# A hybrid retention and attention decoder on one core: column pairs' additions split up, partly given to accumulating DMAs, and an earlier rotary chain

## The chip, the cores and the metric

The kernel runs on one core of a Trainium2 chip. The core has TensorE (PE, matmuls and transposes, with weight loads shown as PEld), VectorE (DVE), ScalarE (ACT) and GpSimd (POOL). SyncE (SP) issues most DMAs. The on-chip memories are SBUF and, for matmul results, PSUM. The metric is the device time of one execution in microseconds (us), lower is better.

## The reference

Two decoder layers work on 256 positions of width 2048, all in fp32. Layer 0 is a retention layer with eight heads, layer 1 is multi-head latent attention (MLA) with 16 heads. Each is followed by a squared-ReLU MLP of width 8192.

```python
for layer in range(DEPTH):
    if layer < N_A_LAYERS:
        h = rms_norm(x, norm_mix[layer])
        x = x + retention(h, ret_w_in[layer], ret_w_out[layer], ret_cos, ret_sin)
    else:
        ...  # shared keys and values once, from the stream after layer 0
        x = x + mla_attention(h, mla_w_dq[j], ..., k_nope, k_pe, v, mla_cos, mla_sin)
    x = x + sq_relu_mlp(rms_norm(x, norm_mlp[layer]), mlp_w1[layer], mlp_w2[layer])

def sq_relu_mlp(h, w1, w2):
    return jnp.square(jax.nn.relu(h @ w1)) @ w2
```

In retention, queries and keys are rotated by tables of sines and cosines of position times frequency:

```python
def rope_tables(positions, dim):
    inv_freq = 1.0 / (ROPE_BASE ** (jnp.arange(0, dim, 2, dtype=jnp.float32) / dim))
    ang = positions.astype(jnp.float32)[..., None] * inv_freq
    return jnp.cos(ang), jnp.sin(ang)
```

## The kernel before

**Matmuls.** Each fp32 operand is split into a high and a low part (`split`, lines 149 to 158). ACT casts the high part, DVE subtracts to get the low part. Three matmuls (high by high, high by low, low by high) make one fp32 product. Weights stream through SBUF in chunks of 1 MB: SP issues the load into one of three `raw` buffers, then ACT and DVE split it in halves into five `wh` and five `wl` buffers, and PE multiplies.

**The program order and the planner.** The Python code runs the steps of a matrix product one chunk at a time. Each chunk ends with `tick()`, which advances a clock by one. Other work is put in a queue with `later(n, fn)` and is written out when the clock reaches its due time (lines 78 to 96). `need` runs queued work early when a list must already have entries. The framework's planner then lays out each engine's instructions, those earlier in program order first where several are ready by its estimates, and adds the waits. On the chip, each engine takes its instructions strictly in that order. SBUF tiles come from small pools; the general pool `f2k` has 14 buffers of 2 KB per partition.

**The start.** The eight halves of the first gate product load their weights and inputs step by step (`start`, lines 539 to 552). After half 3, positions, constants and `gpe` are loaded on SP's queue. After half 5, `ret_tables` (lines 501 to 503) casts the positions on DVE and calls `sincos`, a chain of POOL instructions that reduces the angles to the range of the sine table. `scale_tables` (lines 505 to 515) takes the sine on ACT, multiplies by the row scales of x, and has PE transpose the result (`tr_tp`) into `rope_tab`, with which head 0's queries and keys are rotated.

**The MLP.** The hidden width is worked on in four groups (`mlp`, lines 670 to 726). Of each group there are two up products (`u`) and two down products (`d`) by column pairs of 1024 columns. A column pair (`gemm_pair`) takes eight chunks, called row pairs or quads here, since each holds a 2 by 2 arrangement of blocks. Five quads do eight block products. Three of them, numbers 3, 5 and 7, do seven block products with sums of the weight blocks and of the inputs; DVE makes these sums, so such a quad has fewer matmuls (21 instead of 24) and more DVE work. The seven-product sums end in the PSUM tiles p1, p5, p6 and p7. `pair_out` (lines 332 to 345) brings a pair to its end: six copies by ACT and eight additions by DVE.

For an up pair, `up` (lines 678 to 698) applies the ReLU, and one step later `turn` transposes on PE (`hid_tp`), squares, and splits, which makes four blocks of hidden inputs. For a down pair, `add` (lines 716 to 723) sends four POOL DMAs that accumulate the result into x's home in DRAM (`x_home`). In the last group, the first down pair is instead added to x in SBUF by `done` (`into_next` in layer 0, `finish` in layer 1, both through `add_to_x`, line 415). The last two column blocks then come by plain products (`d_acc`).

**Attention.** After the queries of a block, `query`, `score` and `values` follow one another through `later`. `values` (lines 952 to 959) multiplies by V on PE (`ao`), one step after the transposes of the probabilities are written out (line 948).

Lines that matter below:

```python
                queue.append((clock[0] + 1, -1, lambda: done(pair_out(made, name))))   # 329
        for key, add in (("c11", o["p1"]), ("c12", v), ("c21", u), ("c22", o["p5"])):  # 343
            nc.vector.tensor_tensor(o[key], o[key], add, op=ALU.add)                   # 344
                later(1, turn)                                                         # 698
                            nc.gpsimd.dma_start(x_home[t][b], c[t][j], accum_op=ALU.add)  # 723
            later(1, lambda: values(b, pt))                                            # 948
```

Of the kernel before, what the change touches and what calls it, by code (L numbers as in the profile page):

```python
# [21 lines left out]
NT = 2  # L22
# [28 lines left out]
def yoco(ctx: ExitStack, tc: tile.TileContext, a):  # L51
# [55 lines left out]
    nc.gpsimd.memset(neg_half, -0.5)  # L107
    warm = small(1, "warm")
    nc.scalar.copy(warm, neg_half[:, 0:1])

    dram = ctx.enter_context(tc.tile_pool(name="dr", bufs=1, space=bass.MemoryType.DRAM))
    x_home = [[dram.tile([P, 512], F32, name=f"xh_{t}_{b}") for b in range(NB)] for t in range(NT)]
# [185 lines left out]
    def gemm_pair(w, chunk0, act, kinds, name, done):  # L298

        made = {}  # L300
        total, count = {}, {}
        for seven in kinds:
            for key in ("c11", "c12", "c21"):
                total[key] = total.get(key, 0) + (1 if seven else 2)
            for key in ("p1", "p5", "p6", "p7") if seven else ("c22", "c22"):
                total[key] = total.get(key, 0) + 1

        def get(key):
            if key not in made:
                if key in ("p6", "p7"):  # L310
                    both = two_banks(f"{name}_p67")
                    made["p6"], made["p7"] = both[:, 0], both[:, 1]
                else:
                    made[key] = bank("tp" if key[0] == "p" else "acc", [512], f"{name}_{key}")
            return made[key]

        def mm(key, lhs, rhs):
            dst, n = get(key), count.get(key, 0)
            count[key] = n + 1
            (ah, al), (bh, bl) = lhs, rhs  # L320
            nc.tensor.matmul(dst, ah, bh, start=n == 0, stop=False)  # L321
            nc.tensor.matmul(dst, ah, bl, start=False, stop=False)  # L322
            nc.tensor.matmul(dst, al, bh, start=False, stop=n == total[key] - 1)  # L323

        for i in range(len(kinds)):
            need(act, i + 1)
            quad(w, chunk0 + i, act[i], mm, f"{name}{i}")
            if i == len(kinds) - 1:
                queue.append((clock[0] + 1, -1, lambda: done(pair_out(made, name))))
            tick()  # L330

    def pair_out(c, name):

        o = {}
        for key in ("c22", "c12", "c11", "c21", "p1", "p5"):
            o[key] = f2k([512], f"{name}_{key}")
            nc.scalar.copy(o[key], c[key])
        v, u = (f2k([512], f"{name}_{i}") for i in "vu")
        nc.vector.tensor_tensor(v, c["p6"], o["p1"], op=ALU.add)
        nc.vector.tensor_tensor(u, c["p7"], v, op=ALU.add)  # L340
        nc.vector.tensor_tensor(v, o["p5"], v, op=ALU.subtract)
        nc.vector.tensor_tensor(o["p5"], o["p5"], u, op=ALU.subtract)
        for key, add in (("c11", o["p1"]), ("c12", v), ("c21", u), ("c22", o["p5"])):
            nc.vector.tensor_tensor(o[key], o[key], add, op=ALU.add)
        return [[o["c11"], o["c12"]], [o["c21"], o["c22"]]]

    def with_sums(blocks, name):

# [65 lines left out]

    def add_to_x(acc, b, ss, name):
        for t in range(NT):
            nc.vector.tensor_tensor(x[t][b], acc[t], x[t][b], op=ALU.add)
            if ss is not None:
                square_sum(x[t][b], ss[t][:, b : b + 1], f"{name}_{t}{b}")

# [117 lines left out]

    def start(half):
        first_inputs(half)  # L540
        if half == 3:
            nc.sync.dma_start(pos_i, a["pos"])
            nc.sync.dma_start(cst, a["cst"])
            nc.sync.dma_start(gpe, a["gpe"])
        if half == 5:
            ret_tables()
        if half == 7:
            for b in range(NB):
                later(2 + b, lambda b=b: load_x(b))
            later(5, scale_tables)  # L550
            later(12, lambda: mla_sc.append(sincos(cst[:, C_INVM : C_INVM + 32], 32, "tm")))
            later(20, mla_tables)
# [117 lines left out]
    def mlp(layer, act, r, done):  # L670
        w1, w2 = a[f"mlp_w1_{layer}"], a[f"mlp_w2_{layer}"]
        f0 = 0
        for gi, nf in enumerate(GROUPS):
            hid, blocks = [], []
            kinds = [i in SEVEN for i in range(2 * nf)]
            last = gi == len(GROUPS) - 1

            def up(c, p, hid=hid, blocks=blocks):

                need(r, NT)  # L680
                for t in range(NT):
                    for i in range(2):
                        nc.scalar.activation(c[t][i], c[t][i], AF.Relu, scale=r[t])

                def turn():
                    for q in range(4):
                        name = f"hid{layer}_{p}{q}"
                        tp = transposed(
                            lambda t, j: c[t][q // 2][:, (q % 2 * 2 + j) * P : (q % 2 * 2 + j + 1) * P], f"{name}_tp"
                        )  # L690
                        u = f2k([2, S], f"{name}_u")
                        nc.scalar.activation(u, tp, AF.Square)
                        v = act_tile(name)
                        split_act(v, u)
                        blocks.append((v, with_sums(u, name) if len(blocks) in SEVEN else None))
                        hid.append(v)

                later(1, turn)

            for p in range(f0 // 2, (f0 + nf) // 2):  # L700
                gemm_pair(
                    w1, p * 8, act, [i in SEVEN for i in range(8)], f"u{layer}_{p}", lambda c, p=p, up=up: up(c, p)
                )
            if last:
                x_tiles(lambda t, b: x_home[t][b], f"mlp{layer}")
            for p in range(2):
                if last and p:
                    for b in (2, 3):
                        need(hid, 2 * nf)
                        gemm(  # L710
                            a[f"mlp_w2t_{layer}"], (b - 2) * nf, hid, 4 * nf, 512, f"d{layer}_{gi}{b}",
                            lambda acc, b=b: done(b, acc),
                        )
                    continue

                def add(c, p=p, last=last):
                    for j in range(2):
                        b = 2 * p + j
                        if last:
                            done(b, [c[t][j] for t in range(NT)])  # L720
                            continue
                        for t in range(NT):
                            nc.gpsimd.dma_start(x_home[t][b], c[t][j], accum_op=ALU.add)

                gemm_pair(w2, p * 32 + 2 * f0, blocks, kinds, f"d{layer}_{gi}{p}", add)
            f0 += nf
# [174 lines left out]
    def score(b, qt, qpe):  # L901
# [37 lines left out]
        def turn():  # L939
            pt = []  # L940
            for hh in range(2):
# [3 lines left out]
                o = f2k([3 * P], f"pt{b}{hh}")  # L945
                nc.scalar.copy(o, tp)
                pt.append(o)
            later(1, lambda: values(b, pt))

        later(3, turn)  # L950

# [113 lines left out]
```

## Time and profile before

| what | value |
|---|---|
| median of three runs | 2537.88 us (2533.21 to 2538.45) |
| the profiled execution | 2535.52 us, span of its instructions 2533.7 us |
| mean granted clock of PE | 0.996 |
| PE busy | 2504.2 us, 99% |
| DVE busy | 1912.6 us, 75% |
| ACT busy | 1442.1 us, 57% |
| POOL busy | 180.2 us, 7% |
| moved by DMA | 501.08 MB, mean 198 GB/s |

The page gives busy time by engine. Times in the timeline are microseconds from the first instruction. A row of the timeline has its start, its length, the engine, the line in the kernel, the operation, what it writes and reads, the shapes, the count, and in brackets the idle time of the engine before it with what ended it. A row of the waits has who waited, for whom, the total, the count and the longest. A row of the windows has the stretch, its length, busy time (and count) of PE, PEld, DVE, ACT and POOL, the granted clock, the mean busy share of the 16 DMA engines, and GB/s. A row of the DMA issues has the count, the KB of each and the median time from issue to landing.

### The profile page before, as it was taken

The page shows a single profiled execution, that of the slowest core. Times are in us where ns is not written, and L with a number is a line of the kernel's source. Part 1 is how long each engine was busy: PE and PEld are TensorE (multiplying, and loading weights), DVE is VectorE, ACT ScalarE, POOL GpSimd, SP SyncE. Part 2 cuts the span into 40 slices and gives each one's busy share as a digit, 9 for nine tenths or more (in the row PEclk, how much of TensorE's full clock was granted, in tenths as well). Part 3 has the DMA queues.
Part 4 walks back from the last instruction along what each step waited for, and adds up shares of the span by engine and source line. Part 5 has one row for each costly group of instructions (what it writes and reads, how often), then busy time and mean ns, then how long its engine had stood idle before and what let it go on. Part 6 is the DMA issues. An engine that isn't in the chain of part 4 may idle for free.

```text
span 2533.7 us, 31133 instructions
## 1 busy us (share of the span) xinstructions
PE 2504.2 (99%) x11794; PEld 2092.5 (83%) x11794; DVE 1912.6 (75%) x2478; ACT 1442.1 (57%) x1993; POOL 180.2 (7%) x235
## 2 busy tenths in 40 slices
PE   8999999999999999999999999999999999999998
PEld 6888888888888888788788788998888887888887
DVE  6555555554558888889898756886688889898885
ACT  6444444444446656656566666555566566575663
POOL 6200000000000000000010101110000100000100
PEclk9999999999999999999999999999999999999999
DMA  8455555565665575665675564444655756656754
GB/s 302 165 178 183 185 173 194 174 215 184 206 204 181 189 233 199 215 217 183 218 247 185 203 207 170 162 146 166 197 185 199 233 199 199 224 191 205 261 183 150
DMA packets 82966, 501.08 MB, mean 198 GB/s; under 512 B 9856, under 2 KB 11008, under 8 KB 29568
## 3 DMA queue, kind: packets, MB, share of 16 engines
q1 hardware_dynamic: 71280, 471.78, 53.3%
q0 software_dynamic: 11392, 27.27, 5.0%
q8 instruction: 92, 1.51, 0.2%
q14 instruction: 58, 0.48, 0.1%
q10 hardware_dynamic: 144, 0.05, 0.0%
HBM read 478.09 MB, written 20.97 MB: 197 GB/s over the span
## 4 chain that ended last, share of the span: by engine, by line
PE 73%; DVE 16%; ACT 5%; issue 2%; POOL 2%; DMA 2%; SPq 0%; ACTq 0%; DVEq 0%; POOLq 0%
DVE d_wl L153 7%; PE u_c L322 6%; PE u_c L323 6%; PE u_c L321 6%; PE ro_acc L215 2%; PE ro_acc L214 2%; PE ro_acc L213 2%; PE rv_acc L215 2%; PE rv_acc L213 2%; PE rv_acc L214 2%; ACT d_wh L152 2%; PE rk_acc L241 2%; PE rq_acc L241 2%; PE d_c L322 2%; PE rg_acc L215 2%
## 5 line engine op out<-in xcount | busy, mean ns | idle before, releaser
L153 DVE TENSOR_TENSOR u_wl<-u_raw,u_wh 128x1024 fp32r<-128x1024 f32 (+1 forms) x256 | 278.7, 1118 | 25.7 <-ACT u_wh L152 25.1
L153 DVE TENSOR_TENSOR d_wl<-d_raw,d_wh 128x1024 fp32r<-128x1024 f32 (+1 forms) x256 | 282.1, 1130 | 20.6 <-ACT d_wh L152 20.2
L322 PE MATMUL u_c<-u_wl,n 128*128 128x512 f32 x736 | 287.6, 391 | 0.3 <-DVE u_wl L153 0.2
L321 PE MATMUL u_c<-u_wh,n 128*128 128x512 f32 x736 | 287.4, 390 | 0.0
L323 PE MATMUL u_c<-u_wh,n 128*128 128x512 f32 x736 | 286.4, 389 | 0.0
L152 ACT CAST d_wh<-d_raw 128x1024 fp32r<-128x1024 f32 (+1 forms) x256 | 239.5, 988 | 61.2 <-DMA d_raw<-in_mlp_w 29.9
L152 ACT CAST u_wh<-u_raw 128x1024 fp32r<-128x1024 f32 (+1 forms) x256 | 238.2, 978 | 60.5 <-PE u_c L323 37.0
L322 PE MATMUL d_c<-d_wl,hid 128*128 128x512 f32 x644 | 253.4, 393 | 4.2 <-DVE d_wl L153 4.2
L323 PE MATMUL d_c<-d_wh,hid 128*128 128x512 f32 x644 | 251.0, 390 | 0.0
L321 PE MATMUL d_c<-d_wh,hid 128*128 128x512 f32 x644 | 247.7, 391 | 0.0
L152 ACT CAST u_wh<-u_u 128x1024 fp32r<-128x1024 f32 x96 | 96.6, 1048 | 180.3 <-DVE u_u L286 164.4
L152 ACT CAST d_wh<-d_u 128x1024 fp32r<-128x1024 f32 x84 | 84.0, 1048 | 148.9 <-DVE d_u L286 145.4
L322 PEld LDWEIGHTS u_c<-u_wl,n 128*128 128x128 f32 x736 | 138.2, 188 | 29.5 <-DVE u_wl L153 1.6
L321 PEld LDWEIGHTS u_c<-u_wh,n 128*128 128x128 f32 x736 | 138.2, 188 | 28.5
L323 PEld LDWEIGHTS u_c<-u_wh,n 128*128 128x128 f32 x736 | 138.2, 188 | 28.4
L153 DVE TENSOR_TENSOR u_wl<-u_u,u_wh 128x1024 fp32r<-128x1024 f32 x96 | 113.9, 1222 | 55.0 <-ACT u_wh L152 55.0
L322 PEld LDWEIGHTS d_c<-d_wl,hid 128*128 128x128 f32 x644 | 120.9, 188 | 35.4 <-DVE d_wl L153 8.6
L321 PEld LDWEIGHTS d_c<-d_wh,hid 128*128 128x128 f32 x644 | 120.9, 188 | 25.3
L153 DVE TENSOR_TENSOR ro_wl<-ro_raw,ro_wh 128x1024 fp32r<-128x1024 f32 x64 | 78.4, 1225 | 82.2 <-ACT ro_wh L152 81.9
L323 PEld LDWEIGHTS d_c<-d_wh,hid 128*128 128x128 f32 x644 | 121.0, 188 | 23.3
L153 DVE TENSOR_TENSOR d_wl<-d_u,d_wh 128x1024 fp32r<-128x1024 f32 x84 | 99.2, 1222 | 49.7 <-ACT d_wh L152 49.7
L153 DVE TENSOR_TENSOR rg_wl<-rg_raw,rg_wh 128x1024 fp32r<-128x1024 f32 (+1 forms) x68 | 78.8, 1162 | 63.5 <-ACT rg_wh L152 63.5
(373 smaller groups left out, 6196.5 us busy)
## 6 DMA issues: line engine op xcount, KB each, us to landing
u_raw<-in_mlp_w SPq DMA_DIRECT2D x128, 1024.0 KB, 5.0
d_raw<-in_mlp_w SPq DMA_DIRECT2D x112, 1024.0 KB, 4.9
rv_raw<-in_ret_w_gv SPq DMA_DIRECT2D x32, 1024.0 KB, 4.8
ro_raw<-in_ret_w_out SPq DMA_DIRECT2D x32, 1024.0 KB, 4.9
rg_raw<-in_ret_w_gv SPq DMA_DIRECT2D x28, 1024.0 KB, 4.8
uq_raw<-in_mla_w_uq SPq DMA_DIRECT2D x24, 768.0 KB, 4.3
rq_raw<-in_ret_w_qk SPq DMA_DIRECT2D x16, 1024.0 KB, 4.8
rk_raw<-in_ret_w_qk SPq DMA_DIRECT2D x16, 1024.0 KB, 4.9
```

The lines of the kernel that those rows point to most:

```text
L152: nc.scalar.copy(h, src)
L153: nc.vector.tensor_tensor(l, src, h.bitcast(F32), op=ALU.subtract)
L213: nc.tensor.matmul(acc[t], ah, rh, start=k == 0, stop=False)
L214: nc.tensor.matmul(acc[t], ah, rl, start=False, stop=False)
L215: nc.tensor.matmul(acc[t], al, rh, start=False, stop=k == nk - 1)
L241: nc.tensor.matmul(acc[f], wh[:, cols], a.rearrange("p i s -> p (i s)"), start=k == 0, stop=k == nk - 1)
L321: nc.tensor.matmul(dst, ah, bh, start=n == 0, stop=False)
L322: nc.tensor.matmul(dst, ah, bl, start=False, stop=False)
L323: nc.tensor.matmul(dst, al, bh, start=False, stop=n == total[key] - 1)
```

## The change

- **Start.** Positions and the first 160 columns of `cst` (the frequencies) are loaded by two POOL DMAs at the very beginning. `ret_tables` is called after half 0. The rest of `cst` (mask and identity) and `gpe` are loaded by SP after half 7.
- **Column pairs.** `pair_out` makes its six copies and two additions, and puts a function `rest` in the queue, one row pair later. `rest` makes two more additions and calls `done` with pairs of addends that are not yet added.
- **Up pairs** add them in `summed`, four additions, and transpose in two batches, `turn(0)` in the same step and `turn(1)` one step later.
- **Down pairs** of the first three groups send one accumulating DMA for each addend, eight for a pair. In the last group, block 0 goes to `done` at once and block 1 two steps later, and `add_to_x` adds both addends to x one after the other.
- **Attention.** `values` is due two steps after the transposes, not one.

```diff
@@ -107,6 +107,8 @@
     nc.scalar.copy(warm, neg_half[:, 0:1])
+    nc.gpsimd.dma_start(pos_i, a["pos"])
+    nc.gpsimd.dma_start(cst[:, :C_MASK], a["cst"][:, :C_MASK])
@@ -326,10 +328,10 @@
             if i == len(kinds) - 1:
-                queue.append((clock[0] + 1, -1, lambda: done(pair_out(made, name))))
+                queue.append((clock[0] + 1, -1, lambda: pair_out(made, name, done)))
             tick()
-    def pair_out(c, name):
+    def pair_out(c, name, done):
@@ -338,11 +340,20 @@
         nc.vector.tensor_tensor(v, c["p6"], o["p1"], op=ALU.add)
         nc.vector.tensor_tensor(u, c["p7"], v, op=ALU.add)
-        nc.vector.tensor_tensor(v, o["p5"], v, op=ALU.subtract)
-        nc.vector.tensor_tensor(o["p5"], o["p5"], u, op=ALU.subtract)
-        for key, add in (("c11", o["p1"]), ("c12", v), ("c21", u), ("c22", o["p5"])):
-            nc.vector.tensor_tensor(o[key], o[key], add, op=ALU.add)
-        return [[o["c11"], o["c12"]], [o["c21"], o["c22"]]]
+
+        def rest():
+            nc.vector.tensor_tensor(v, o["p5"], v, op=ALU.subtract)
+            nc.vector.tensor_tensor(o["p5"], o["p5"], u, op=ALU.subtract)
+            done([[(o["c11"], o["p1"]), (o["c12"], v)], [(o["c21"], u), (o["c22"], o["p5"])]])
+
+        later(1, rest)
+
+    def summed(c):
+
+        for row in c:
+            for block in row:
+                nc.vector.tensor_tensor(block[0], block[0], block[1], op=ALU.add)
+        return [[block[0] for block in row] for row in c]
@@ -414,7 +425,8 @@
         for t in range(NT):
-            nc.vector.tensor_tensor(x[t][b], acc[t], x[t][b], op=ALU.add)
+            for part in acc[t] if isinstance(acc[t], tuple) else (acc[t],):
+                nc.vector.tensor_tensor(x[t][b], part, x[t][b], op=ALU.add)
@@ -538,13 +550,11 @@
         first_inputs(half)
-        if half == 3:
-            nc.sync.dma_start(pos_i, a["pos"])
-            nc.sync.dma_start(cst, a["cst"])
-            nc.sync.dma_start(gpe, a["gpe"])
-        if half == 5:
+        if half == 0:
             ret_tables()
         if half == 7:
+            nc.sync.dma_start(cst[:, C_MASK:], a["cst"][:, C_MASK:])
+            nc.sync.dma_start(gpe, a["gpe"])
@@ -678,12 +688,13 @@
                 need(r, NT)
+                c = summed(c)
...
-                def turn():
-                    for q in range(4):
+                def turn(i):
+                    for q in (2 * i, 2 * i + 1):
...
-                later(1, turn)
+                later(0, lambda: turn(0))
+                later(1, lambda: turn(1))
@@ -717,10 +729,11 @@
                         if last:
-                            done(b, [c[t][j] for t in range(NT)])
+                            later(2 * j, lambda b=b, j=j: done(b, [c[t][j] for t in range(NT)]))
                             continue
                         for t in range(NT):
-                            nc.gpsimd.dma_start(x_home[t][b], c[t][j], accum_op=ALU.add)
+                            for part in c[t][j]:
+                                nc.gpsimd.dma_start(x_home[t][b], part, accum_op=ALU.add)
@@ -945,7 +958,7 @@
-            later(1, lambda: values(b, pt))
+            later(2, lambda: values(b, pt))
```

## The prediction

> **What bounds the kernel now.** I read the page's busy times first, then TensorE's list of waits, then the timeline around each wait, then the DMA views.
>
> ```profile
> span 2533.7 us, 31133 instructions
> PE 2504.2 (99%) x11794; PEld 2092.5 (83%) x11794; DVE 1912.6 (75%) x2478; ACT 1442.1 (57%) x1993; POOL 180.2 (7%) x235
> ...
> PE 73%; DVE 16%; ACT 5%; issue 2%; POOL 2%; DMA 2%; SPq 0%; ACTq 0%; DVEq 0%; POOLq 0%
> ```
> ```profile
> PE rg_acc L213 <- ACT a L155: 5.8, 1, 5.8
> PE d_acc L214 <- DVE d_wl L153: 4.5, 3, 2.9
> PE ao L955 <- ACT pt L946: 4.2, 3, 2.9
> PE d_c L322 <- DVE d_wl L153: 4.2, 7, 0.7
> PE tr_tp L172 <- DVE tr_scaled L510: 3.9, 2, 3.3
> ```
>
> TensorE (PE) computes for 2504 of 2534 us, so no edit that keeps the matmuls can win more than the idle rest. The wait list says where that rest is: 5.8 us before the first matmul, which the edit leaves alone, and some 17 us at a few places in the middle. The edit aims at all of these. The chain names DVE with 16%: for long stretches DVE is only just ahead of PE, and this decides what a lump of DVE work costs. An idle row understates its price, because PE restarts slowly:
>
> ```profile
> 57.97 0.39 PE L214 MATMUL rv_acc<-rv_wl,a 128*128 128x512 f32 x1
> 61.70 0.48 PE L172 MATMUL tr_tp<-cst,tr_scaled 128*128 128x128 f32 x1 [3.33 <-DVE tr_scaled L510]
> 62.77 0.90 PE L172 MATMUL tr_tp<-cst,tr_scaled 128*128 128x128 f32 x3 [0.60 <-DVE tr_scaled L510]
> ...
> 63.90 0.63 PE L213 MATMUL rv_acc<-rv_wh,a 128*128 128x512 f32 x1
> 64.32 0.63 PE L214 MATMUL rv_acc<-rv_wl,a 128*128 128x512 f32 x1
> ...
> 67.25 0.39 PE L215 MATMUL rv_acc<-rv_wh,a 128*128 128x512 f32 x1
> 67.48 0.39 PE L213 MATMUL rv_acc<-rv_wh,a 128*128 128x512 f32 x1
> ```
>
> Matmuls start every 0.23 us at full pace (67.25, 67.48), but every 0.42 us for a while after this idle time (63.90, 64.32). From 57.97 to 67.25 stand ten matmuls and four short transposes, some 2.3 + 0.4 us at full pace; 9.3 us passed. So this one wait cost 6.6 us, not 3.9.
>
> **Part 1: rotary chain at once.** Positions and the first 160 columns of `cst` come by two GpSimd DMAs at the start, and `ret_tables` runs after the first input piece instead of the sixth. The rest of `cst` and `gpe` move on SP's queue from half 3 to half 7.
>
> ```profile
> 15.80 1.84 POOL L444 TENSOR_SCALAR tr_ang<-cst,pos_f 128x128 f32<-128x128 f32 x2 [14.96 <-DVE pos_f L502]
> ...
> 56.64 0.62 POOL L471 TENSOR_SCALAR tr_rr<-tr_rr 128x512 f32<-128x512 f32 x1
> ```
> ```profile
> 55.26 1.30 POOL tr_rr L460
> 56.58 3.81 DMA x<-in_x
> ```
> ```profile
> gains<-in_gains ACTq DMA_DIRECT2D x1, 49.0 KB, 3.5
> pos_i<-in_pos SPq DMA_DIRECT2D x1, 1.0 KB, 6.8
> ```
>
> POOL's chain runs 41.5 us without a pause, 15.80 to 57.26. Both things that `tr_scaled` needs hang on its end: the sine, and the last loads of x, which get their buffer when POOL's temporary is freed (the chain of waits goes from POOL to that DMA). A small load on a quiet queue landed in 3.5 us, one behind SP's weights in 6.8. Issued at about 0.8 us, the positions land between 4.3 and 7.6 us, so POOL starts some 8 to 9 us sooner. The transposes were late by 3.7 us (57.97 to 61.70), so the wait goes: 6.4 us of the 6.6. Late next are the scaled tables, at 61.7 - 8.5 = 53.2 us, still 4.8 ahead of PE. POOL has nothing else to do until x's scales. The cast of the positions stands in DVE's queue ahead of the next weight split. By the slower landing it could hold this, and PE behind it, for up to 3 us; by the faster one nothing. SP loses one small issue there and moves two behind the first eight input pieces, ahead of the next weights: up to 1 us either way. I take 0 for both, nearer to the faster row, since that queue too is empty.
>
> By the Trainium skill's page "TensorE: Matmul & The Clock Gate", Part 1, the clock halves only after an idle window of about 3.4 us. By that this wait would give back 4.4 us instead of 6.4; the trace disagrees, slow matmuls follow 3.33 us of idle time here, and 2.91 us in part 2.
>
> **Part 2: additions in lumps.** At the end of a column pair DVE made eight additions at once. Now two are made at once; two come after the next row pair ("quad"). The last four are made there too for the up projection, are folded into the sum with x for the last group, and are left to accumulating DMAs for the other down pairs.
>
> ```profile
> 890.50 1.07 PE L321 MATMUL d_c<-d_wh,hid 128*128 128x512 f32 x4
> 892.24 0.50 PE L322 MATMUL d_c<-d_wl,hid 128*128 128x512 f32 x1 [0.67 <-DVE d_wl L153]
> 892.58 0.40 PE L323 MATMUL d_c<-d_wh,hid 128*128 128x512 f32 x1
> ```
> ```profile
> 887.96 0.68 DVE L341 TENSOR_TENSOR d_v<-d_p,d_v 128x512 f32<-128x512 f32 x1
> ...
> 890.98 4.62 DVE L153 TENSOR_TENSOR d_wl<-d_raw,d_wh 128x1024 fp32r<-128x1024 f32 x4
> ```
>
> An addition occupies DVE for 0.6 us in sequence (five from 887.96 to 890.98). Between the two down pairs of a group, the second quad's split waits for those five, and PE for the split: 892.24 should have been 891.41, plus 0.11 at the next, 0.94 us. Three of the five go, so the split starts 1.8 us earlier and the wait goes. Six such places (three groups, two layers): 5.6 us.
>
> At the last group the lump holds the additions to x too:
>
> ```profile
> 2486.21 0.61 PE L213 MATMUL d_acc<-d_wh,hid 128*128 128x512 f32 x2
> 2489.74 0.50 PE L214 MATMUL d_acc<-d_wl,hid 128*128 128x512 f32 x1 [2.91 <-DVE d_wl L153]
> ...
> 2490.89 0.63 PE L213 MATMUL d_acc<-d_wh,hid 128*128 128x512 f32 x1
> ...
> 2494.18 0.40 PE L215 MATMUL d_acc<-d_wh,hid 128*128 128x512 f32 x1
> ```
> ```profile
> 1408.32 0.87 PE L172 MATMUL n_tp<-cst,x_mlp 128*128 128x128 f32 x6 [0.56 <-DVE x_mlp L417]
> 1410.65 0.50 PE L214 MATMUL d_acc<-d_wl,hid 128*128 128x512 f32 x1 [1.46 <-DVE d_wl L153]
> ```
>
> Layer 1: 3.1 us lost up to 2489.74, 0.2 at the next, 1.5 in eight slow matmuls (2490.89 to 2494.18, 3.3 us for 1.8): 4.8. Before the second quad's split stand twelve additions; block 1's four are put off by two pieces, so eight remain, 2.4 us less. About 0.7 us of wait remains and no slow matmuls: gain 4.1. Layer 0 waited 0.56 + 1.46; the same shift covers the second: gain 2.0 with its restart. Sum 6.1, bounded by 0 and 8.2.
>
> For up pairs the count of additions is unchanged and DVE had already split the next quad when they began; PE's list of waits names neither `hid_tp` nor more than 0.2 us of `u_c`. I take 0, with 0.94 x 16 pair ends = 15 us either way as the bound. The MLP transposes in two batches keep their number; their blocks are first read four quads later, 21 us, so this is 0 too.
>
> The DMA part costs. Twelve down pairs send eight accumulations instead of four:
>
> ```profile
> xh<-d_c POOLq DMA_DIRECT2D x48, 256.0 KB, 7.0
> ```
> ```profile
> 866.00:880.00 14.00, 14.00 (x64) 11.42 (x63) 12.62 (x14) 5.98 (x8) 0.00 (x0) 1.00 0.65 225
> 886.00:904.00 18.00, 17.33 (x77) 13.86 (x76) 15.53 (x19) 8.45 (x10) 3.47 (x4) 1.00 0.93 253
> ```
> ```profile
> 1239.03 9.54 DMA d_raw<-in_mlp_w
> ```
> ```profile
> 1251.08 0.50 PE L322 MATMUL d_c<-d_wl,hid 128*128 128x512 f32 x1 [0.17 <-DVE d_wl L153]
> ```
>
> Weights alone keep the DMA engines 0.65 busy for 225 GB/s, 2.9 us for a MB. With four accumulations in 886 to 904 the share is 0.93, 16.7 us; of 4.55 MB moved 1.05 are theirs, so the weights took 10.1 us and an accumulation some 1.65. Four more are 6.6 us in each pair of 183 matmuls x 0.227 = 41.5 us, which has 0.35 x 41.5 = 14.5 us free and uses 6.6 of it now. So they fit, but locally: a weight load took 9.54 us, and PE lost 0.17 us of idle time by it. The second addend of a block must wait until the first has landed (7.0 us by the row). Behind that wait on POOL stand only further accumulations and, in the last group, loads of x that only the end of the last down pair needs. This wait spreads the DMAs out, and the first ones, copies that need no addition, start sooner. Eight of 14 buffers stay held for two landings, some 14 us; the next pair needs eight again 41 us on. Price: between 0 and 12 x 6.6 = 79 us. I take 0.3 per pair, 4 us, near the rows above, where four accumulations cost 0 to 0.4.
>
> **Part 3: values one piece later.**
>
> ```profile
> 1658.61 0.70 PE L955 MATMUL ao<-pt,v 128*128 128x256 f32 x2 [1.05 <-ACT pt L946]
> ...
> 1659.78 0.70 PE L955 MATMUL ao<-pt,v 128*128 128x256 f32 x2 [0.25 <-ACT pt L946]
> ```
>
> These 1.3 us go, with 0.1 of restart: 1.4. The longest such wait, 2.9 us, is head 7's, where `need` forces the steps in the same order whatever their due time; I leave it.
>
> **Sum.** 6.4 + 5.6 + 6.1 + 1.4 - 4 = 15.5. The profiled execution took 2535.5 us (span 2533.7), 2.4 below the median of 2537.9 and inside the runs, 2533.2 to 2538.5. So 2520.
>
> **Rivals.** (A) Weights starve. While accumulations are pending, the weights get about 10.1 of 16.7 us, one MB in 5.2 us, just PE's own pace (41.5 / 8); eight keep this up twice as long, and the reserve, already gone at 1251, cannot refill. If half of the added 6.6 us shows, 40 us are lost against 19.5 gained: 2555. It decides from 1.6 us per pair. For it: the 9.54 us load. Against: the weights' share sufficed so far. The Trainium skill's page "DMA: Bandwidth & Descriptors", section "Queues, rings and completion order", has the engines take turns between queues packet by packet, which speaks for this rival; the trace agrees that both progress together.
>
> (B) The planner lays the instructions out anew, and the lumps meet other splits a quad later: parts 1 and 3 hold, part 2 gives nothing: 2535.5 - 7.8 + 4 = 2532. For it: DVE is 92% busy in 842.9 to 891:
>
> ```profile
> 842.90:891.00 48.10, 48.00 (x218) 38.52 (x217) 44.17 (x58) 32.96 (x45) 2.08 (x3) 1.00 0.56 185
> ```
>
> Against: 48 additions vanish, 29 us of DVE.
>
> (C) The early chain does not do what it says: the positions land late and DVE's wait for them eats the gain, so part 1 gives 0: 2526.
>
> **Chances.** Forecast 0.50 (2509 to 2528), C 0.08, B 0.18, A 0.20, and 0.04 beyond the low end. What counts as no change is 0.2%, 5 us. B lies at its edge; I give half of it to "same" and count 0.01 of A there. Faster 0.71, same 0.10, slower 0.19. The range, 2508 to 2544, holds the forecast, C, B and the milder half of A.
>
> **What would show it.** Right: `tr_ang` starts before 9 us and no `tr_tp` wait over 0.5 us; no d_c L322 wait of 0.67 between down pairs; 96 rows of `xh<-` accumulations; the DVE total down by about 29 us; no 0.42 us spacing near 2490; the 2.9 us `ao` wait still there. Wrong: weight loads of over 10 us followed by waits of PE or ACT on DMA, PE waiting on `hid_tp` by over 0.5 us, or a DVE wait on the positions before 8 us.

## The result and the profile after

The changed kernel takes 2528.3 us (median of 22 runs, 2523.44 to 2535.35), the kernel before 2536.12 us on the same chips (22 runs, 2532.94 to 2538.64). The ratio is 0.9973, 95% interval [0.9966, 0.998]: 7.8 us or 0.3% faster. The forecast was 2520 us, 15.5 us faster, about twice that gain. The profiled execution has a span of 2530.4 us.

From the page of the changed kernel, the span, TensorE's busy time and the chain of waits:

```profile
span 2530.4 us, 31172 instructions
...
PE 2498.0 (99%) x11794; PEld 2096.4 (83%) x11794; DVE 1889.2 (75%) x2430; ACT 1445.9 (57%) x1993; POOL 220.6 (9%) x285
...
PE 84%; DVE 8%; DMA 4%; ACT 3%; issue 1%; POOL 1%; SPq 0%; ACTq 0%; DVEq 0%; POOLq 0%
```

TensorE's waits in the changed kernel (who waits, for whom, total, count, longest):

```profile
PE rg_acc L215 <- ACT a L157: 12.0, 2, 6.8
PE u_c L324 <- DVE u_wl L155: 5.2, 4, 2.2
PE d_c L324 <- DVE d_wl L155: 3.7, 5, 1.0
PE tr_tp L174 <- DVE tr_scaled L522: 1.9, 2, 1.2
PE d_acc L216 <- DVE d_wl L155: 1.4, 2, 0.9
PE qptp L174 <- DVE ot L155: 1.3, 2, 0.8
PE qptp L174 <- ACT qt L904: 1.2, 1, 1.2
```

Read against the list of before, it shows most of the story. `tr_tp`, `d_acc` and `ao` shrank. `rg_acc` grew from 5.8 to 12.0, so a second long wait has appeared in the first product. `u_c`, which was not among the long waits, now stands second. And the `d_c` waits add up to nearly as much as before (3.7 us against 4.2), though the ones in the forecast are gone: none of the five lies in the second quad of a pair, they come some 22 us after its first matmul.

Comparing when the same matmul starts in the two traces gives the balance by stage: up to the scores of head 0 the changed kernel loses 8.2 us, in the MLP of layer 0 it wins 2.6, in the attention 4.2, in the MLP of layer 1 4.5. So the rotary part lost more than it was to win, and the other two parts together won 11.3 (forecast: 9.1). (These are two single executions, 3.3 us apart in their spans; the medians are 7.8 apart.)

**The loss at the start.** Timeline of the changed kernel, SP's issues, ACT and TensorE:

```profile
3.54 8.48 SPq L192 DMA_DIRECT2D rg_raw<-in_ret_w_gv  x5
12.06 2.98 SPq L535 DMA_DIRECT2D x0t<-in_xt  x6
...
17.13 3.30 ACT L157 ACTIVATE a<-x0t,gains 128x256 fp32r<-128x256 f32 x8 [1.51 <-DMA x0t<-in_xt]
...
17.69 0.79 PE L215 MATMUL rg_acc<-rg_wh,a 128*128 128x512 f32 x1 [6.76 <-ACT a L157]
...
19.71 0.80 PE L217 MATMUL rg_acc<-rg_wh,a 128*128 128x512 f32 x1 [0.80 <-DVE a L158]
20.30 0.63 PE L215 MATMUL rg_acc<-rg_wh,a 128*128 128x512 f32 x1
20.73 0.63 PE L216 MATMUL rg_acc<-rg_wl,a 128*128 128x512 f32 x1
```

And SP's issues in the kernel before:

```profile
1.17 0.42 SPq L523 DMA_DIRECT2D x0t<-in_xt  x1
1.64 0.90 SPq L190 DMA_DIRECT2D rg_raw<-in_ret_w_gv  x2
2.58 0.43 SPq L523 DMA_DIRECT2D x0t<-in_xt  x1
3.06 0.43 SPq L190 DMA_DIRECT2D rg_raw<-in_ret_w_gv  x1
3.53 0.59 SPq L523 DMA_DIRECT2D x0t<-in_xt  x1
```

Before, SP alternates between weights and the inputs `x0t` that go with them. Now six of the eight input pieces are issued together at 12.06, behind nine weight pieces, the last of which waited 2.6 us for an earlier load to land and 2.6 us for DVE to free a buffer. ACT waits for the input, TensorE for ACT, 6.76 us, and then it works at half pace, one matmul every 0.42 us, up to 24 us. The first `rq` matmul comes at 40.56 instead of 29.73.

### The profile page after: what moved, and what is told of

Its sections match the earlier page's. It is cut to its first block, busy times and chain, and to the rows that moved or that the text cites. A ratio compares the mean times of both kernels' runs of the same rounds, so it can differ in the third digit from the quotient of the medians.

```text
span 2530.4 us, 31172 instructions
## 1 busy us (share of the span) xinstructions
PE 2498.0 (99%) x11794; PEld 2096.4 (83%) x11794; DVE 1889.2 (75%) x2430; ACT 1445.9 (57%) x1993; POOL 220.6 (9%) x285
## 4 chain that ended last, share of the span: by engine, by line
PE 84%; DVE 8%; DMA 4%; ACT 3%; issue 1%; POOL 1%; SPq 0%; ACTq 0%; DVEq 0%; POOLq 0%
PE u_c L324 6%; PE u_c L325 6%; PE u_c L323 6%; PE d_c L324 5%; PE d_c L325 5%; PE d_c L323 5%; PE rq_acc L243 2%; PE rg_acc L217 2%; PE ro_acc L217 2%; PE ro_acc L215 2%; PE ro_acc L216 2%; PE rg_acc L215 2%; PE rg_acc L216 2%; PE rv_acc L216 2%; PE rv_acc L217 2%; PE rv_acc L215 2%
## 5 line engine op out<-in xcount | busy, mean ns | idle before, releaser
L155 DVE TENSOR_TENSOR d_wl<-d_raw,d_wh 128x1024 fp32r<-128x1024 f32 (+1 forms) x256 | 283.5, 1133 | 28.1 <-ACT d_wh L154 27.1
L324 PEld LDWEIGHTS d_c<-d_wl,hid 128*128 128x128 f32 x644 | 121.0, 188 | 31.2 <-DVE d_wl L155 6.8
```

The costliest lines, as they stand in the source:

```text
L155: nc.vector.tensor_tensor(l, src, h.bitcast(F32), op=ALU.subtract)
```

## The experiments

My theory after the comparison: (1) part 1 loses because the rotary chain, called after half 0, takes its six buffers from the general pool ahead of `x0t_1` and the following, in program order, so that the planner lays their loads out late; (2) the second four accumulations of a down pair cost 10 us and more, not 4; (3) everything else wins more than I forecast. "The first, third, fourth ... kernel" in the expectations are the runs in the order below. Each is given as its median, and its ratio to the kernel before on the same chip.

**1. Parts 2 and 3 alone.** The start as before.

```diff
-        if half == 0:
-            ret_tables()
+        if half == 3:
+            nc.sync.dma_start(pos_i, a["pos"])   # and cst, gpe
+        if half == 5:
+            ret_tables()
```

> The changed kernel with the start put back as it was before: parts 2 and 3 alone. Theory (part 1 costs 8 us, because the inputs x0t_1 to x0t_6 come behind nine weight pieces in SP's queue; parts 2 and 3 together win about 11): about 11 us faster than before, 2525 where before is 2536, and TensorE's first rq matmul back near 29.7 us. Rival (the late inputs come from something else in the change, for example the values or the lumps): no faster than the changed kernel, 8 us below before.

Measured: 2524.46 us, 0.9953 [0.994, 0.9965]. Without part 1 the change is 3.8 us faster than with it, and 11.4 us faster than before, as the theory had it; the first `rq` matmul is at 30.42 us.

**2. Part 1 alone**, on the kernel before.

> The kernel before with part 1 alone. Theory (part 1 costs about 11 us at the first matmul and wins back 2 to 3 at the rotary transposes): about 8 us slower than before, with ACT waiting for DMA x0t near 17 us. Rival (the loss at the start is given back in the MLP, where everything is later by it): within 3 us of before. The prediction's own sum for this part: 6 us faster.

Measured: 2540.92 us, 1.0022 [1.0014, 1.0031], 5.1 us slower than before. TensorE waits 12.2 us for ACT's `a`, as in the changed kernel. Between the theory's 8 and the rival's 3, and with the sign opposite to the forecast's.

**3. The chain's buffers taken and written at once.** The six temporaries are allocated together, and each gets a one-column memset, so that the pool's order no longer puts `x0t` behind the chain's late instructions.

```diff
+        k, kh, kl, r, part = (f2k([2, n], f"{name}_{i}") for i in ("k", "kh", "kl", "rr", "part"))
+        if name == "tr":
+            for i in (ang, k, kh, kl, r, part):
+                nc.gpsimd.memset(i[:, 0, 0:1], 0.0)
```

> The changed kernel with one more edit: the six temporaries of the rotary chain are taken from the pool at once and each is written by a one-column POOL memset (six short instructions more), so that the input tiles after them in the pool's order need not be laid out behind the chain. Theory (the loads are late because their buffers come after the chain's last temporary in the pool's order): SP issues x0t_1 to x0t_7 between the first weight pieces as before, TensorE's first rq matmul at or below 30 us, some 10 us faster than the changed kernel, 2517 to 2520 where that is at 2528. Rival (the early loads of the positions on POOL's queue, or the raw buffers, make them late): the same time as the changed kernel, within 3 us.

Measured: 2523.22 us, 0.995 [0.9935, 0.9964], 5.1 us faster than the changed kernel. SP alternates again, so the order of buffers was the cause of the late loads. But the first `rq` matmul is at 35.13 us, not 30: half of that delay stays, although the time is run 1's again. DVE and TensorE in this kernel:

```profile
17.46 3.07 DVE L158 SCALAR_TENSOR_TENSOR a<-x0t,gains,a 128x256 fp32r<-128x256 f32 x4
...
19.04 0.50 PE L217 MATMUL rg_acc<-rg_wh,a 128*128 128x512 f32 x1 [0.95 <-DVE a L158]
```

The same instructions in the kernel before, ahead of POOL's chain (which begins at 15.80) and during it:

```profile
10.41 1.67 DVE L156 SCALAR_TENSOR_TENSOR a<-x0t,gains,a 128x256 fp32r<-128x256 f32 x4
...
23.97 3.06 DVE L156 SCALAR_TENSOR_TENSOR a<-x0t,gains,a 128x256 fp32r<-128x256 f32 x4
```

Four of them take 1.67 us while POOL is idle and 3.06 while it computes, and this stood in the trace of before. A crowd of loads is not the difference: in that trace the DMA engines are full in both stretches (a busy share of 1.03 from 10.4 to 12.1 us and 0.99 from 23.9 to 27.1). At 24 us PE has work ahead that covers it; at the very start it has none, and TensorE waits for `a`.

**4. Last additions by DVE, a quad later, four accumulations** (start as before).

```diff
                 def add(c, p=p, last=last):
+                    if not last:
+                        c = summed(c)
...
-                            for part in c[t][j]:
-                                nc.gpsimd.dma_start(x_home[t][b], part, accum_op=ALU.add)
+                            nc.gpsimd.dma_start(x_home[t][b], c[t][j], accum_op=ALU.add)
```

> Parts 2 and 3 alone (as the first of these), but a down pair's last four additions are made by DVE again, a quad later than before, and it sends four accumulating DMAs as before. Theory (the second four accumulations cost about 1 us per pair through slower weight loads, 10 to 12 us in all): 5 to 10 us faster than parts 2 and 3 with eight accumulations; weight loads near the pairs' ends back below 8 us. Rival (DVE is the bound there, as the prediction has it, and the 48 additions, 29 us of DVE, pay): 3 to 6 us slower than with eight accumulations, with waits of d_c on d_wl of 0.5 us and more at the pairs' ends.

Measured: 2513.05 us, 0.9911 [0.9897, 0.9924]: 22.8 us faster than before and 11.4 faster than run 1, a little more than the theory's 5 to 10. The DMA form of the additions costs 11.4 us net, 0.95 per down pair. The 48 additions that DVE makes again leave no wait of `d_c` among TensorE's waits in this kernel:

```profile
PE rg_acc L213 <- ACT a L155: 5.4, 1, 5.4
PE tr_tp L172 <- DVE tr_scaled L520: 3.5, 2, 2.9
PE u_c L322 <- DVE u_wl L153: 1.6, 3, 1.0
PE d_acc L214 <- DVE d_wl L153: 1.3, 2, 0.9
```

Where the DMA price sits is seen from the time of each column pair, from its first matmul to the next pair's first (worked out from the starts in the traces; means, us). The last row goes from the first to the last `d_acc` matmul:

| pair | before | changed | run 4 | run 7 (below) |
|---|---|---|---|---|
| second up pair of a group (8) | 43.43 | 43.28 | 43.28 | 43.50 |
| first down pair (8) | 44.27 | 43.53 | 43.50 | 44.23 |
| second down pair (6) | 42.60 | 42.43 | 41.78 | 42.55 |
| first up pair after a down pair (6) | 41.67 | 42.92 | 41.90 | 41.69 |
| last group's end, layers 0 and 1 | 49.47, 48.59 | 47.17, 44.53 | 47.15, 44.55 | 48.05, 47.83 |

In the changed kernel the pairs during and after the accumulations are longer than in run 4: 6 x 0.65 and 6 x 1.0 = 10 us. The stretch from 886 to 914 us, behind a first down pair, as rows of the windows; first before, then changed, then run 4 (the accumulations begin at 885.9, 889.8 and 885.5):

```profile
886.00:914.00 28.00, 27.33 (x121) 22.14 (x120) 24.34 (x28) 13.92 (x16) 3.47 (x4) 1.00 0.83 245
```
```profile
886.00:914.00 28.00, 27.77 (x123) 22.67 (x121) 21.90 (x24) 17.54 (x22) 7.08 (x8) 1.00 0.98 272
```
```profile
886.00:914.00 28.00, 28.00 (x124) 22.93 (x123) 25.55 (x29) 15.10 (x17) 3.06 (x4) 1.00 0.88 263
```

With eight accumulations the DMA engines are 0.98 busy for 28 us, with four 0.83 to 0.88. The weights get what is left. Two waits of TensorE in the changed kernel, the second with what DVE did before it:

```profile
914.45 0.50 PE L324 MATMUL d_c<-d_wl,hid 128*128 128x512 f32 x1 [0.68 <-DVE d_wl L155]
...
1307.39 1.23 DVE L283 TENSOR_TENSOR u_u<-u_raw 128x1024 f32<-128x1024 f32 x1 [4.42 <-DMA u_raw<-in_mlp_w]
...
1310.54 0.50 PE L324 MATMUL u_c<-u_wl,n 128*128 128x512 f32 x1 [2.21 <-DVE u_wl L155]
```

The list of waits names DVE for both, but in the second case the cause is seen to be a weight load: DVE idles 4.42 us for `u_raw`, and TensorE then 2.21 us for DVE. Ahead of the first, ACT had idled 4.86 us up to 902.47 for a `d_raw` load; that the wait at 914.45 follows from it is argued.

**5. Four more accumulations that do not depend on each other**, into a spare array, which four plain DMAs fill first.

```diff
                             nc.gpsimd.dma_start(x_home[t][b], c[t][j], accum_op=ALU.add)
+                            nc.gpsimd.dma_start(spare[t][j], c[t][j], accum_op=ALU.add)
```

> The fourth kernel (parts 2 and 3 with the start of before, last additions of the down pairs by DVE, four accumulations, 2513 us) plus four more accumulating DMAs per down pair of the first three groups, of the same finished sums into a spare array in DRAM that nothing reads: the bytes of the change, without the second addend's wait for the first one's landing. (The spare array is first filled by four plain DMAs.) Theory (the second four cost DMA time that the weights need): 6 to 12 us slower than the fourth kernel, 2519 to 2525, with weight loads of 8 us and more near the pairs' ends. Rival (what costs is the wait of the second addend for the first, and the buffers held by it): within 3 us of 2513.

Measured: 2535.68 us, 1.0004 [0.9994, 1.0013]: 22.6 us slower than run 4, twice the changed kernel's price and beyond the theory's 6 to 12. So it is the transfers that cost. The wait of the second addend for the first, in the changed kernel, spreads them: the first eight are issued over 13.5 us there (889.8 to 903.3) and over 7.4 us here. That this makes them cheaper is argued, not shown, since DVE makes the additions too in this run. The waits of TensorE and, in the timeline, the last accumulation that a pair issues:

```profile
PE u_c L323 <- DVE u_wl L154: 11.8, 9, 2.2
```
```profile
893.15 2.50 POOL L741 DMA_DIRECT2D sp<-d_c  x1
```

This one landed at 912.50, 19.35 us after its issue, and the weight loads issued from 893 to 901 took 8.5 to 10.0 us.

**6. The transposes of an up pair in one batch** again, on run 4.

```diff
-                later(0, lambda: turn(0))
-                later(1, lambda: turn(1))
+                later(1, lambda: (turn(0), turn(1)))
```

> The fourth kernel with all four MLP transposes of an up pair in one batch, a quad later, as before. Theory (the batch of transposes cost TensorE 0.24 and 0.19 us at each end of an up pair before, and 0.16 in two batches): 2 to 4 us slower than the fourth kernel, 2515 to 2517. The prediction's step (0 for the transposes): within 1 us of 2513.

Measured: 2516.14 us, 0.9922 [0.9909, 0.9936]. The median is 3.1 us above run 4's, but the intervals overlap. The trace is sharper: the second up pairs take 43.56 us here and 43.28 in run 4, 2.2 us in eight, the first down pairs 0.06 each more, and the ends of the last groups are 1.0 us shorter in sum. So the two batches win 1 to 2 us, where the prediction had 0.

**7. All eight additions in one lump** again, on run 4.

```diff
-        later(1, rest)
+        rest()
```

> The fourth kernel with the eight additions of a column pair again in one lump (rest at once, not a quad later); block 1 of the last group stays put off. The prediction's step (a lump between two down pairs costs 0.94 us, six of them, plus part of the last groups): 5.6 to 9 us slower than the fourth kernel, with d_c waiting 0.6 to 0.7 us for d_wl in the second quad. Rival (the lump was not the cause, the accumulations around it were): within 2 us.

Measured: 2530.13 us, 0.9978 [0.9969, 0.9987]: 17.1 us slower than run 4, above both forecasts. TensorE's waits:

```profile
PE d_c L322 <- DVE d_wl L153: 4.1, 6, 0.7
...
PE d_acc L214 <- DVE d_wl L153: 3.5, 2, 2.6
```

The six waits of 0.7 between down pairs are back. The table under run 4 tells the rest: the second down pairs lose 0.77 each (4.6 in all), the last groups 4.2, and the first down pairs 0.73 each, eight of them, 5.8 us, where the lump belongs to the up pair before. The second up pairs lose 0.22 each, 1.8.

**8. Values one step after the transposes**, part 3 undone, on run 4.

```diff
-            later(2, lambda: values(b, pt))
+            later(1, lambda: values(b, pt))
```

> The fourth kernel with the attention's values one step after the transposes, as before: part 3 undone. By the shift of the stages the attention won 4.2 us, not 1.4, and the 2.9 us wait of ao went with it. Theory (one step later is what removed that wait too): 4 us slower, 2517, with ao waits of 2.7 to 2.9 us. The prediction's step (head 7 keeps its order whatever the due time): 1.4 us slower, 2514.5, and no such wait comes back.

Measured: 2519.05 us, 0.9933 [0.992, 0.9945], 6.0 above run 4; the profiled execution, however, had a span of 2511.6, 0.6 below run 4's. The wait of 2.9 us is back. See run 14.

**9. Run 3 with the additions by DVE** (the whole change, both faults mended).

> The third kernel (whole change, the chain's six temporaries written at once) with the last additions of the down pairs by DVE, as in the fourth. Theory (the early chain, its loads in order, wins as much at the rotary transposes as DVE loses at the start, because DVE's instructions take 0.79 us instead of 0.48 while POOL computes): within 2 us of the fourth kernel's 2513. Rival (early chain in order is a plain gain of up to 6 us, the prediction's part 1): 2507 to 2509.

Measured: 2514.1 us, 0.9917 [0.9904, 0.993], as run 4. With its loads in order the early chain neither wins nor loses: the first `rq` matmul is 5.0 us later than in run 4, and from the scores of head 0 on the two differ by 0.7.

**10. The chain begun in between.** Positions and the first columns of `cst` on SP's queue after half 2, the rest as run 9.

```diff
+        if half == 2:
+            nc.sync.dma_start(pos_i, a["pos"])
+            nc.sync.dma_start(cst[:, :C_MASK], a["cst"][:, :C_MASK])
+        if half == 4:
+            ret_tables()
```

> As the kernel before it in this list, but positions and the first columns of cst are loaded by SP after half 2 (before the change: after half 3), so that the chain begins some 3 to 4 us sooner than before the change and some 4 us later than with the change. Theory: DVE is slowed only once TensorE has work ahead, the rotary transposes wait less: 1 to 4 us faster than the fourth kernel, 2509 to 2512. Rival (the wait at the transposes is set by the loads of x, not by the chain): within 1 us of it.

Measured: 2512.63 us, 0.9913 [0.9899, 0.9927]: not to be told from run 4. In the trace POOL starts at 13.11, the first `rq` matmul is at 29.96, and the wait at the transposes is shorter:

```profile
PE tr_tp L172 <- DVE tr_scaled L519: 1.9, 2, 1.3
```

The scores of head 0 start 2.7 us earlier than in run 4. A gain of 2 us is likely, but the times don't show it.

**11, 12, 13. POOL busy at the start with work of its own**, on run 4, the orders of the other engines unchanged.

```diff
+    idle = pool.tile([P, 128], F32, tag="idle", bufs=1, name="idle")
+    for _ in range(30):      # run 11: 14; run 12: 45 times memset(idle, 0.5)
+        nc.gpsimd.tensor_scalar(idle, idle, 0.5, 0.25, op0=ALU.mult, op1=ALU.add)
```

> The fourth kernel plus fourteen POOL instructions at the very start that read and write a small tile of their own (128 x 128, tensor_scalar), some 8 to 13 us of POOL that nobody waits for; the orders of the other engines stay as they are. Theory (DVE and POOL share a way to SBUF: DVE instructions of two SBUF inputs are slowed by POOL's): before 12 us DVE's a takes 0.7 to 0.8 us instead of 0.48 and its 512-column split 1.0 to 1.2 instead of 0.69, and TensorE's first rq matmul comes 1 to 4 us later. Rival (DVE was slowed in the changed kernel by the crowd of loads, not by POOL): durations as in the fourth kernel, no later.

> The fourth kernel plus 45 POOL memsets of the same small tile at the very start, which write only. Theory: if only POOL's reads are in DVE's way, DVE's durations stay at 0.48 and 0.69 us and the time at 2513; if its writes are too, they rise as with the reading instructions.

> As the eleventh kernel, with thirty of the POOL instructions that read and write, so that POOL computes until 13 us or later, while DVE makes the first splits and inputs. Theory (POOL's reads are in the way of DVE instructions with two SBUF inputs): between 9 and 13 us DVE's a takes 0.6 to 0.8 us instead of 0.48 and its 512-column split over 0.9 instead of 0.69, as behind the chain; the first rq matmul up to 3 us later. Rival (small reads are not in DVE's way, or the crowd of loads was): 0.48 and 0.69 us as in the fourth kernel.

Measured: 2514.45, 2512.86 and 2514.82 us (0.9916 [0.9902, 0.993], 0.9912 [0.9898, 0.9926], 0.9916 [0.9902, 0.9929]); the times are not apart. Run 11 answers nothing: its POOL work ended at 6.8 us, when DVE had hardly begun. Timelines, first of run 12 (writes only), then of run 13 (reads and writes):

```profile
1.04 11.77 POOL L113 MEMSET idle<- 128x128 f32 x45
...
10.48 1.66 DVE L160 SCALAR_TENSOR_TENSOR a<-x0t,gains,a 128x256 fp32r<-128x256 f32 x4
```
```profile
1.07 15.05 POOL L113 TENSOR_SCALAR idle<-idle 128x128 f32<-128x128 f32 x30
...
11.54 1.80 DVE L160 SCALAR_TENSOR_TENSOR a<-x0t,gains,a 128x256 fp32r<-128x256 f32 x4
13.26 2.70 DVE L157 TENSOR_TENSOR rg_wl<-rg_raw,rg_wh 128x512 fp32r<-128x512 f32 x3
```

Writes leave DVE as fast as an idle POOL does (1.66 us for four). Reads slow it: 1.80 for four, 2.70 for three splits, 0.90 each, for which run 4 needs 2.48; the first `rq` matmul comes 1.6 us later than in run 4, at 31.81 (the kernels with the start of before lie between 29.7 and 31.2). The effect is smaller than the theory's, and than with the chain's instructions of 512 columns (3.07 for four), but there is one, and without any change in the loads.

**14. Run 8's kernel again.**

> The eighth kernel (values one step after the transposes, all else as the fourth) once more. If values one step later are worth 4 us and more, the median lies again near 2519 and the profiled run shows, behind the 2.9 us wait of ao, matmuls at 0.42 us; if they are worth 1.4 us, near 2514.5, and the first median was the chip's scatter.

Measured: 2516.81 us, 0.9925 [0.9911, 0.9939]; span 2515.5. The two profiles of this one kernel differ behind the same wait. Run 8:

```profile
1727.12 0.70 PE L969 MATMUL ao<-pt,v 128*128 128x256 f32 x2 [2.91 <-ACT pt L960]
...
1728.11 0.40 PE L214 MATMUL wo_acc<-wo_wl,ot 128*128 128x512 f32 x1
1728.34 0.40 PE L215 MATMUL wo_acc<-wo_wh,ot 128*128 128x512 f32 x1
```

Run 14:

```profile
1726.54 1.22 PE L969 MATMUL ao<-pt,v 128*128 128x256 f32 x2 [2.87 <-ACT pt L960]
...
1728.41 0.63 PE L214 MATMUL wo_acc<-wo_wl,ot 128*128 128x512 f32 x1
1728.84 0.63 PE L215 MATMUL wo_acc<-wo_wh,ot 128*128 128x512 f32 x1
```

After 2.91 us of idle time matmuls start every 0.23 us, at a granted clock of 1.00; after 2.87 us they start every 0.43 us for 4 us more, at 0.50. This price of 2.8 us (from the first `ao` to the same matmul, at 1730.42 and 1732.65) comes in some executions and not in others. It explains part of the distance between run 8's profile and its median, not all.

**15. Part 3 alone**, on the kernel before.

> The kernel before with part 3 alone. The prediction's step: 1.4 us faster than before. Theory (the 2.9 us wait of ao and the slow matmuls after it go too, new waits of qptp of 2.5 us come): 3 to 4.5 us faster, with ao waits below 0.5 us and qptp waits of 1.2 us in their place.

Measured: 2532.88 us, 0.9988 [0.998, 0.9997]: 2.5 us faster than before, between the two forecasts. The 2.9 us wait is gone; in its place stand

```profile
PE qptp L172 <- DVE ot L153: 1.9, 2, 1.4
PE qptp L172 <- ACT qt L891: 1.2, 1, 1.2
```

By the starts of the matmuls the attention wins 3.7 us in this profile.

## Why the prediction was wrong in size

As a whole, the sign was right and the time lay inside the range, but the gain was half of the 15.5 us in the sum, because part 1 came out with the other sign. In the other terms larger gains and a larger price cancelled.

- **Part 1: +6.4 forecast, a loss of 5.1 us measured (run 2; 3.8 inside the whole change, run 1).** The step that failed is "SP loses one small issue there and moves two behind the first eight input pieces ... I take 0 for both". It counted the DMAs that the edit itself moves on SP's queue, and not those that it pushes: `ret_tables` earlier in program order takes six buffers of the pool that the inputs `x0t` share, and TensorE waits for these inputs, 12.0 us where it had been 5.8. Mending that alone gives back 5.1 us (run 3); the scores of head 0 then start at 82.03 us, in run 1 at 82.07, in the changed kernel at 89.31. Rival C, which gave part 1 a value of 0, had another cause: the positions landed in time (`tr_ang` at 7.73 us).
- **"POOL has nothing else to do"** was true, and beside the point: DVE is slower while POOL computes, which the trace of before showed. This is why the gain of 6.4 us doesn't come even with the loads in order (run 9 against run 4: none): run 3's first `rq` matmul is 4.7 us later than run 1's, and what the transposes win back is just that. Runs 12 and 13 support that POOL's reads are the cause; that they are the whole of the 4.7 us is argued from the instructions' durations, not shown.
- **"Late next are the scaled tables, at 53.2 us, still 4.8 ahead of PE"**: no. Next were the last loads of x. The changed kernel's timeline, SP's issue and ACT's use:

```profile
58.09 0.87 SPq L548 DMA_DIRECT2D x<-in_x  x2
...
67.06 0.63 ACT L149 ACTIVATE n_sq<-x 128x512 bf16<-128x512 f32 x1 [0.46 <-DMA x<-in_x]
```

  The early chain freed its buffer, but SP issues these loads in its order among the weights, and they take 9 us; `tr_tp` still waited 1.9 us though the first of these transposes came 7.7 us later than before (69.35 against 61.70).
- **Lumps between down pairs: 5.6 forecast, 4.9 measured** (second down pairs, 42.60 to 41.78, run 4). Right, with its mechanism: run 7 brings the waits of 0.7 back. In the changed kernel the extra DMAs' price hides most of it.
- **Last groups: 6.1 forecast, 6.3 measured** (2.3 and 4.0). The mechanism is right, the closeness is partly luck. In the trace of before, matmuls at half pace follow the wait of 2.91 us in layer 1, and the prediction counts them. Runs 2 and 15, whose MLP is that of before, wait 2.9 us there too and go on at full pace: their last groups' ends take 48.9 and 47.1 us, and against these run 4 wins 4.4 (1.8 and 2.6).
- **Up pairs: "I take 0"; 6.2 us measured.** The first down pairs are 0.77 us shorter (44.27 to 43.50, eight of them), and run 7 shows that `rest` a quad later did it. By the starts of the matmuls, 0.37 us of it stands by the end of the third quad, around the transposes, which move with `rest`, and 0.28 more in the fourth; the lump itself and the place of the transposes are not separated. I had read the list of waits, where delays of 0.2 us don't show, and let the bound of 15 us stand beside it without going to the starts of the matmuls. For the same reason "no edit that keeps the matmuls can win more than the idle rest" doesn't hold: run 4's span is 21.5 us shorter (2533.7 to 2512.2), and 11.6 of these had been counted as PE's busy time (2504.2 to 2492.6).
- **The DMA term: 4 us forecast, 11.4 measured** (run 4 against run 1; 0.95 per pair against 0.3). The working of rival A had the mechanism: the weights' share during accumulations, the 9.54 us load. Its price came to 0.95 us per pair, below the 1.6 from which it decides. I took the cost that I had read off for the first four, 0 to 0.4, for that of the second four, though by rival A's own working the reserve was gone by then.
- **Part 2 as a whole**, with its DMAs, won 7.1 us by the stages (2.6 and 4.5; forecast 11.7 - 4 = 7.7). So rival B, by which it gives nothing, falls; but the forecast's net is near by luck, both of its errors being some 7 us.
- **Part 3: 1.4 forecast, 2.5 measured.** The claim that head 7's wait of 2.9 us would remain because `need` forces the order was wrong: it went with the one step (runs 8, 15), and new waits for `qptp`, which were not forecast, took its place. By the starts of the matmuls, the attention takes 379.3 to 379.9 us in all kernels with part 3. Without it, it takes 380.8 in run 8 and 381.1 in run 2, but 383.5 in run 14 and 383.6 before, where half pace follows the wait of 2.9 us. So the part wins the forecast's 1.4 in some executions and some 4 in others.

Of the signs that I named: `tr_ang` before 9 us, no `d_c` wait in the second quad between down pairs, 96 accumulations, no 0.42 us spacing near 2490, all seen. The `tr_tp` waits over 0.5 us and PE waits behind late weight loads were seen too, the ones named as wrong, though no load took over 10 us (the longest 9.88). So was a DVE wait for the positions, 0.88 us up to 5.21, but the first matmul is not later for it (5.26 against 5.78). DVE's total fell by 23.4 us, not 29. Run 1, with the late chain, has 1887.3 us and run 4, which makes the 48 additions again, 1912.5: they are worth 25.2 us, 0.52 each and not 0.6, and the early chain costs DVE 1.9.

What would have been better: run 4 keeps part 3 and the split lumps, has DVE make the additions, and leaves the start alone. At 0.9911 [0.9897, 0.9924] it wins three times what the change does. Run 10 is its equal.

## What to carry to other kernels

When a block of code is moved earlier, list the pool buffers that it takes and who stands behind it for the same pool, not only the DMAs that it issues. Here four more transfers per pair, through DMA engines that were already 0.83 busy in that stretch, cost 0.95 us a pair net, so the saving on DVE (48 additions, 25 us), which is not the bound there, did not pay for them. Price an added transfer by the busy share of its stretch. For delays that repeat at every pair, measure the pairs from first matmul to first matmul; the list of waits leaves out those that are short.

## What the runs showed of the hardware

- DVE instructions with two inputs in SBUF take up to 1.8 times as long while POOL's rotary chain computes (3.06 against 1.67 us for four in the kernel before), 1.08 times beside short POOL instructions that read (1.80, run 13), and as long as ever while POOL only writes (1.66, run 12). The Trainium skill's page "SBUF — State Buffer", section "Who interferes with whom", says this: the second input of such a DVE instruction comes through the read port that it shares with GpSimd, so it contends with GpSimd's reads and not with its writes. Runs 12 and 13 agree.
- The half clock after an idle time of 2.9 us comes in one execution and not in the next (granted clock 0.50 in run 14, 1.00 in run 8). The Trainium skill's page "TensorE: Matmul & The Clock Gate", Part 1, has a free-running window, so that the outcome depends on where in it the idle time falls; that agrees with the two traces, while its figure for the window, about 3.4 us, is longer than the 2.87 us after which run 14's clock had halved.
- Accumulating DMAs of 256 KB, sent eight at a time beside a stream of weights, take up to 19.35 us to land (run 5), and 22.6 us of the kernel's time for 48 of them.
